# New engine orders for the head and the first ten units of a one-core matmul-tanh-mul kernel, and the sums of one pair and a cast of the next moved later behind them

## The chip, the cores and the metric

One core of a Trainium2 chip. The metric is device time in microseconds (us) of one execution. Every run told of here is of the fast state. Ratios are computed as the mean time of one kernel's fast runs over that of the other's fast runs of the same rounds, so they are not quite the ratio of the medians that are quoted beside them. Engines: PE is TensorE, DVE is VectorE, ACT is ScalarE, SP is the sync engine that issues most DMAs (198 of the 204 that the page of the kernel before lists).

## The reference

```python
batch, m, k, n = 16, 512, 1024, 768        # x: (16, 512, 1024), w1, w2: (1024, 768), float32
y1 = np.matmul(x, w1)
y2 = np.matmul(x, w2)
return (np.tanh(y1) * y2).astype(np.float32)
```

## The kernel before

The 64 x tiles of 128 rows are worked in two ways. The first six tiles ("head") are multiplied directly in bf16 as the weights arrive: matmul `m20F3` is tile 2, weight 0 (called a; weight 1 is b), the wide 512 columns (`G` are the other 256), block 3 of the contraction. The other 58 tiles are 29 pairs. A pair and a weight make a unit of seven fp16 products (four matmuls each) on sums and differences of blocks, instead of eight. DVE and ACT make these sums (`s1` to `s4` of x; `t1` to `t4` and `b11` to `b22` of the weights), scale and cast x (`cx`), and combine products (`c12`, `c22`, seeds, which ACT copies from one bank to another, tanh, final multiply). Fillers are matmuls on a constant tile whose result nobody uses.

The program fixes the order of each engine's instructions. In the traces DVE started its listed casts, blocks, sums, c and multiplies in that order (the first 96 of them, behind which the later units mix in). The orders of the head and of the first ten units stand in the kernel as lists, found by a search; later units are placed by a formula in slots of 0.65 us, one product each.

```python
    FILL = {"m00F0": 3, "m00F1": 6}          # filler matmuls ahead of these two
    ORDER = {
        "pe": """ T00 T01 m00F0 m00G0 T10 T11 m00F1 m00G1 m10F0 T20 ... """,
        "act": """ ... tanh4F tanh5F ax10 ax11 tanh4G ax20 cx11 b11b b22b seed.0 seed.1 ... """,
        "dve": """ ... """, "dma": """ ... """,
    }
    # ... cut ...
    def feed(n, bank=banks[3]):
        for _ in range(n):
            pin(nc.tensor.matmul(bank[:, :2 * P], ones.bitcast(bf16)[:, :P], ones.bitcast(bf16), start=True, stop=True))
    # ... cut ...
    "c12": ("dve", 0.55, 3, ["p3", "u2"], add_out, (u, "d", "u2", "c12")),
    "c22": ("dve", 0.55, 4, ["p7", "s5"], add_out, (u, "b", "s5", "c22")),
    "p4": ("pe", 0.65, 6, ["c22"], unit_product, (u, "p4", "b", False, True)),   # waits for c22
    # ... cut: behind the planned part; FIRST is 6, the seventh pair ...
    for i in range(FIRST, PAIRS):
        z = 14 * i - 6
        at(slot(z - 7), blocks, i)
        for j, n in enumerate(("s1", "s2", "s3", "s4")):
            at(slot(z - 5.5 + 1.3 * j), s_block, i, n, "dve")
        # ... cut ...
        late = 1.1 * (i == FIRST + 1)
        at(slot(z - 25 + late), scale_x, i)
        for h in range(2):
            at(slot(z - 24 + late + 4 * h), cast_x, i, h, "dve")
            at(slot(z - 24 + late + 4 * h), transpose_x, i, h)
```

## Time and profile before

| | before |
|---|---|
| median of the first six runs | 317.22 us (316.65 to 317.68) |
| span of the profiled run | 315.3 us |
| PE, DVE, ACT busy | 98%, 78%, 73% |
| starts that PE loses to waits after 5.12 us | about 2.3 us |

"Starts lost" is the useful measure here: it is the distance between two starts in PE's order of time, less the pace of that shape (0.163 us for 384 columns, from four in 0.65, and 0.216 for 512, from 22 in 4.75, both in the trace of the kernel before). The prediction says why, and shows the lines.

### The profile page before, as it was taken

Reading aid. Unit: us, or ns where it says so; the run is one execution under the profiler, and the core shown is the slowest. Engines: PE = TensorE matmul, PEld = TensorE weight load, DVE = VectorE, ACT = ScalarE, POOL = GpSimd, SP = SyncE. Lnnn points to the kernel's source line nnn. Section 1 sums busy time; section 2 is a strip of 40 time slices with the busy share of each in tenths; the row PEclk is TensorE's granted clock in tenths of the full one; section 3 lists DMA queues with packets and bytes.
Section 4 is the critical chain, followed back from the end, with each engine's and each line's share of the span. In section 5 each row is a group of like instructions: output and inputs, shape, how many; then the busy total and the mean of one; then the engine's idle time right before and its main releaser. Section 6 shows DMA issues by size and latency. Waiting matters only on the chain.

```text
span 315.3 us, 5481 instructions
## 1 busy us (share of the span) xinstructions
PE 307.9 (98%) x1890; PEld 185.5 (59%) x1895; DVE 244.8 (78%) x571; ACT 230.5 (73%) x453; POOL 4.3 (1%) x10
## 2 busy tenths in 40 slices
PE   8999999999998999999999999999999999999994
PEld 5756656666555555555555556555555555555652
DVE  2688978888887778877777897777789777777743
ACT  3788789786887777778777777877777778876551
POOL 0000000000000000000000000000000000000003
PEclk9999999999999999999999999999999999999998
DMA  7999498999999998999999989999998899996222
GB/s 289 406 400 369 95 311 245 262 263 264 308 318 267 287 278 258 246 231 287 268 255 242 285 239 224 299 252 283 242 251 265 263 246 282 234 238 168 101 101 102
DMA packets 82300, 80.59 MB, mean 256 GB/s; under 512 B 63584, under 2 KB 64096, under 8 KB 82272
## 3 DMA queue, kind: packets, MB, share of 16 engines
q1 hardware_dynamic: 81408, 78.27, 89.0%
q10 hardware_dynamic: 864, 1.97, 1.6%
q8 instruction: 15, 0.25, 0.3%
q14 instruction: 13, 0.11, 0.1%
HBM read 39.85 MB, written 25.17 MB: 206 GB/s over the span
## 4 chain that ended last, share of the span: by engine, by line
PE 86%; DMA 6%; DVE 3%; ACT 2%; issue 1%; DVEq 0%; SPq 0%; ACTq 0%
PE bank L401 79%; PE bank L267 4%; DMA x_f<-in_x_dram 3%; DMA xT<-x_h 3%; PE bank L270 2%; PE bank L223 1%; ACT junk L340 1%; DVE x_h L360 1%; DVE o L287 1%; DVE t L318 1%; ACT b L313 0%; DVE c L423 0%; DVE o L437 0%; ACT x_h L362 0%; DVE t L322 0%
## 5 line engine op out<-in xcount | busy, mean ns | idle before, releaser
L401 PE MATMUL bank<-t,s 128*128 128x384 f16 x696 | 131.6, 326 | 0.4 <-DVE t L318 0.4
L401 PEld LDWEIGHTS <-s 128*128 128x128 f16 x928 | 90.6, 98 | 61.1 <-issue 0.8
L401 PEld LDWEIGHTS <-xT 128*128 128x128 f16 x696 | 67.9, 98 | 48.0 <-issue 2.2
L401 PE MATMUL bank<-b,xT 128*128 128x384 f16 x464 | 93.8, 326 | 0.2 <-ACT b L313 0.2
L423 DVE TENSOR_TENSOR c<-bank,u 128x384 f32<-128x384 f32 x58 | 32.0, 554 | 43.6 <-PE bank L401 41.1
L340 ACT ACTIVATE junk<-x_f 128x1024 bf16<-128x1024 f32 x58 | 60.8, 1049 | 2.6 <-DMA x_f<-in_x_dram 2.5
L431 ACT ACTIVATE th<-c,out_r 128x384 f32<-128x384 f32 x58 | 35.3, 609 | 21.9 <-DVE c L423 21.9
L401 PE MATMUL bank<-t,xT 128*128 128x384 f16 x232 | 47.0, 326 | 0.8 <-DVE c L423 0.8
L401 PE MATMUL bank<-b,s 128*128 128x384 f16 x232 | 47.1, 327 | 0.0
L418 ACT ACTIVATE u<-bank 128x384 f32<-128x384 f32 x58 | 28.2, 487 | 19.7 <-PE bank L401 19.3
L360 DVE TENSOR_SCALAR x_h<-x_f,pr 128x1024 f16<-128x1024 f32 x55 | 41.0, 747 | 0.2
L414 ACT ACTIVATE bank<-bank 128x384 f32<-128x384 f32 x58 | 27.8, 481 | 12.7 <-DVE o L437 10.1
L423 DVE TENSOR_TENSOR c<-bank,s 128x384 f32<-128x384 f32 x58 | 32.2, 555 | 6.0 <-PE bank L401 5.0
L431 ACT ACTIVATE th<-bank,out_r 128x384 f32<-128x384 f32 x58 | 33.3, 573 | 4.5 <-PE bank L401 4.5
L437 DVE SCALAR_TENSOR_TENSOR o<-bank,out_r,th 128x384 f32<-128x384 f32 x58 | 35.4, 611 | 0.9 <-PE bank L401 0.9
L437 DVE SCALAR_TENSOR_TENSOR o<-c,out_r,th 128x384 f32<-128x384 f32 (+1 forms) x57 | 34.3, 606 | 0.4 <-ACT th L431 0.2
L418 ACT ACTIVATE s<-bank 128x384 f32<-128x384 f32 x58 | 27.8, 482 | 7.3 <-PE bank L401 5.0
L382 DVE TENSOR_TENSOR s<-xT 128x512 f16<-128x512 f16 x58 | 24.1, 417 | 0.1
L267 PE MATMUL bank<-wb,xTb 128*128 128x512 bf16 x91 | 23.9, 380 | 0.2
L270 PE MATMUL bank<-wb,xTb 128*128 128x256 bf16 x96 | 14.6, 273 | 0.0
L260 ACT ACTIVATE junk<-wf 128x768 bf16<-128x768 f32 (+1 forms) x13 | 12.8, 988 | 1.4 <-DMA wf<-in_w_dram 1.2
L267 PEld LDWEIGHTS <-xTb 128*128 128x128 bf16 x96 | 9.3, 99 | 7.5 <-DVE xTb L231 0.3
(49 smaller groups left out, 144.3 us busy)
## 6 DMA issues: line engine op xcount, KB each, us to landing
x_f<-in_x_dram SPq DMA_DIRECT2D x64, 512.0 KB, 6.0
out_dram<-o SPq DMA_DIRECT2D x62, 384.0 KB, 3.7
wf<-in_w_dram SPq DMA_DIRECT2D x12, 384.0 KB, 8.2
wf<-in_w_dram ACTq DMA_DIRECT2D x4, 384.0 KB, 7.8
xT<-x_h SPq DMA_TRANSPOSE x58, 3.9
out_dram<-o ACTq DMA_DIRECT2D x2, 192.0 KB, 2.1
out_dram<-o SPq DMA_DIRECT2D x2, 192.0 KB, 2.4
```

The source lines that it names most:

```text
L260: pin(nc.scalar.activation(junk[:, :n * N].rearrange("p (k n) -> p k n", n=N), w_f[t][:, k:k + n, :], ACT.Abs, accum_out=asum_w[t][:, j:j ...
L267: pin(nc.tensor.matmul(bank, hx[mt][:, k, :], w_b[t][k][:, :F], start=k == 0, stop=k == KO - 1))
L270: pin(nc.tensor.matmul(bank[:, at_:at_ + G], hx[mt][:, k, :], w_b[t][k][:, F:], start=k == 0 and mt % 2 == 0, stop=k == KO - 1, skip_group ...
L340: pin(nc.scalar.activation(junk[:, :K], xs[HEAD + 2 * i + h], ACT.Abs, scale=2.0 ** -12, accum_out=pair_sum[i][:, h:h + 1]))
L360: pin(nc.vector.tensor_scalar(xh, xs.pop(mt), pair_r[i][:, h:h + 1], None, ALU.mult))
L382: pin((nc.vector if eng == "dve" else nc.gpsimd).tensor_tensor(s, st[i, a], st[i, b], op))
L401: pin(nc.tensor.matmul(bank[:, cols], st[i, a][:, k, :], wt[t][b][:, k, cols], start=start and k == 0, stop=stop and k == KH - 1, skip_gro ...
L414: pin(nc.scalar.activation(ub[u]["b"][:, :Q], ub[u]["a"][:, :Q], ACT.Copy))
L418: pin(nc.scalar.activation(c, ub[u][bank][:, :Q], ACT.Copy))
L423: pin(nc.vector.tensor_tensor(c, ub[u][bank][:, :Q], ub[u][other], ALU.add))
L431: pin(nc.scalar.activation(th, v, ACT.Tanh, scale=rs[i][:, 0, h:h + 1]))
L437: pin(nc.vector.scalar_tensor_tensor(o[:, h, q * Q + cols.start:q * Q + cols.stop], v, rs[i][:, 1, h:h + 1], tanhs[i, h, q][:, cols], ALU. ...
```

## The change

A longer search gave new orders for all engines in the head and the first ten units, and three formulas behind them were shifted. No real work is added or removed; two filler matmuls are added, and some casts and evacuations change their engine. The intent is to remove PE's remaining waits.

```diff
-        "e01": "dve", "e11": "dve", "e20": "act", "e21": "dve", "e31": "dve", "ca0": "act", "ca1": "act",
-        "cb4": "act", "b22a": "dve", "cx11": "act", "cx31": "act", "cx61": "act"
+        "e10": "act", "e21": "dve", "e31": "dve", "cb4": "act", "b22a": "dve", "cx11": "act", "cx31":
+        "act", "cx41": "act", "cx61": "act"
-    FILL = {"m00F0": 3, "m00F1": 6}
+    FILL = {"m00F0": 8, "m10F0": 3}
 PE's list, cut to what matters later:
-   ... suma m11F0 m20F6 m20F7 m01F0 m00G5 m00G6 m00G7 m11F1 m01F1 m30F0 ... m30F7 m21F0 m21F1 m11F2 ...
+   ... suma m20F5 m10G6 m10G7 m30F0 m20F6 m20F7 m11F0 m11F1 m11F2 m01F0 m01F1 m01F2 m31F0 m31F1 m31F2
+   m00F7 m30F1 ... m30F7 m11F3 ...
 ACT's list, cut:
-   ... tanh4F tanh5F ax10 ax11 tanh4G ax20 cx11 b11b b22b seed.0 seed.1 ...
+   ... tanh4F ax10 tanh5F ax11 tanh4G b22b b11b cx11 seed.0 ax21 s5.0 seed.1 u2.0 ax20 ...
 (the rest of the four lists is cut)
-            at(slot(z - 5.5 + 1.3 * j), s_block, i, n, "dve")
+            at(slot(z - 5.5 + 1.6 * (i == FIRST) + 1.3 * j), s_block, i, n, "dve")
-            at(slot(z - 24 + late + 4 * h), cast_x, i, h, "dve")
-            at(slot(z - 24 + late + 4 * h), transpose_x, i, h)
+            at(slot(z - 24 + (1 + h) * late + 4 * h), cast_x, i, h, "dve")
+            at(slot(z - 24 + (1 + h) * late + 4 * h), transpose_x, i, h)
```

More of the change, by code (lines that the diff above doesn't have):

```diff
@@ L58 @@
     ELSEWHERE = {
-        "e01": "dve", "e11": "dve", "e20": "act", "e21": "dve", "e31": "dve", "ca0": "act", "ca1": "act",
-        "cb4": "act", "b22a": "dve", "cx11": "act", "cx31": "act", "cx61": "act"
+        "e10": "act", "e21": "dve", "e31": "dve", "cb4": "act", "b22a": "dve", "cx11": "act", "cx31":
+        "act", "cx41": "act", "cx61": "act"
     }
-    FILL = {"m00F0": 3, "m00F1": 6}
+    FILL = {"m00F0": 8, "m10F0": 3}
     ORDER = {
         "pe": """
-            T00 T01 m00F0 m00G0 T10 T11 m00F1 m00G1 m10F0 T20 m10G0 m10G1 m10F1 T21 m20G0 m20F0 m20F1 m20G1
-            m10G2 m20G2 m00F2 m00G2 m20F2 m10F2 T30 T31 m10G3 m00G3 m20F3 m10F3 m20G3 m00F3 m10F4 m10G4 m20F4
-            m20G4 m00G4 m00F4 m30G0 m30G1 m30G2 m30G3 m20G5 m10G5 m10F5 m20F5 m20G6 m10G6 m10F6 m30G4 m30G5
-            m30G6 m20G7 m10G7 m30G7 m10F7 m00F5 m00F6 m00F7 suma m11F0 m20F6 m20F7 m01F0 m00G5 m00G6 m00G7
-            m11F1 m01F1 m30F0 m30F1 m30F2 m30F3 m30F4 m30F5 m30F6 m30F7 m21F0 m21F1 m11F2 m21F2 m01F2 m11F3
-            m21F3 m01F3 m31F0 m31F1 m31F2 m31F3 m21G0 m21G1 m21G2 m21G3 m31G0 m31G1 m31G2 m31G3 m01F4 m31G4
-            m21G4 m11F4 m01G0 m01G1 m11G0 m11G1 m01G2 m01G3 m01G4 m31F4 T4 m11F5 m11F6 m01F5 m31F5 m01G5 m01G6
-            m31F6 m01F6 m31G5 m31G6 m01F7 m31F7 m11F7 m31G7 T5 m40F0 m40F1 m40F2 m40F3 m40F4 m40F5 m40F6 m01G7
-            m40F7 m21G5 m21G6 m50F0 m50F1 m50F2 m50F3 m50F4 m50F5 m50F6 m50F7 m21F4 m21F5 m21G7 m21F6 m21F7
-            m11G2 m11G3 m11G4 m11G5 m11G6 m11G7 m40G0 m50G0 m50G1 m50G2 m50G3 m50G4 m50G5 m50G6 m50G7 m40G1
-            m40G2 m40G3 m40G4 m40G5 m40G6 m40G7 sumb m41F0 m41F1 m41F2 m41F3 m41F4 m41F5 m41F6 m41F7 m41G0
-            m41G1 m41G2 m41G3 m41G4 m41G5 m41G6 m51G0 m51G1 m51G2 m51G3 m51G4 m51G5 m51G6 m51G7 m41G7 m51F0
-            m51F1 m51F2 m51F3 m51F4 m51F5 m51F6 m51F7 p1.0 p1.1 p5.0 p6.0 p2.0 p3.0 p7.0 p5.1 p6.1 p4.0 p2.1
-            p7.1 p1.2 p3.1 p4.1 p1.3 p6.2 p2.2 p5.2 p6.3 p2.3 p5.3 p7.2 p7.3 p3.2 p4.2 p3.3 p4.3 p1.4 p1.5
-            p5.4 p5.5 p2.4 p6.4 p6.5 p2.5 p7.4 p7.5 p3.4 p3.5 p4.4 p4.5 p1.6 p1.7 p5.6 p6.6 p2.6 p6.7 p2.7
-            p7.6 p3.6 p5.7 p7.7 p4.6 p3.7 p1.8 p4.7 p1.9 p2.8 p6.8 p5.8 p5.9 p7.8 p1.10 p3.8 p4.8 p3.9 p6.9
@@ new lines @@
+            T00 T01 m00F0 m00G0 T10 T11 m10F0 m10G0 m10G1 m00G1 m10F1 m00F1 T20 T21 m00F2 m10G2 m00G2 m10F2
+            m20F0 T30 m20F1 m20G0 m20F2 m20G1 m20G2 T31 m20G3 m20F3 m00G3 m00F3 m10F3 m20G4 m00F4 m10F4 m00G4
+            m20F4 m30G0 m30G1 m30G2 m30G3 m00G5 m00F5 m30G4 m30G5 m20G5 m00F6 m20G6 m00G6 m30G6 m30G7 m20G7
+            m00G7 m10G3 m10G4 m10F5 m10F6 m10F7 m10G5 suma m20F5 m10G6 m10G7 m30F0 m20F6 m20F7 m11F0 m11F1
+            m11F2 m01F0 m01F1 m01F2 m31F0 m31F1 m31F2 m00F7 m30F1 m30F2 m30F3 m30F4 m30F5 m30F6 m30F7 m11F3
@@ new lines @@
+            m11F4 m01F3 m01F4 m31F3 m21G0 m31G0 m21G1 m21G2 m21G3 m21G4 m01G0 m01G1 m01G2 m01G3 m01G4 m11G0
+            m11G1 m21F0 m21F1 m21F2 m21F3 T4 m21F4 m21G5 m01G5 m01G6 m01F5 m11F5 m01F6 m01F7 m21G6 m21G7 m11G2
+            m11G3 m11G4 m11G5 m11G6 m31G1 m31G2 m31G3 m40F0 m40F1 m21F5 m21F6 m21F7 m11F6 m11F7 T5 m31F4 m31F5
+            m31F6 m31F7 m40F2 m40F3 m40F4 m40F5 m40F6 m40F7 m50F0 m50F1 m50F2 m50F3 m50F4 m50F5 m40G0 m40G1
+            m40G2 m50G0 m11G7 m01G7 m50F6 m50F7 m40G3 m40G4 m40G5 m40G6 m40G7 m31G4 m31G5 m50G1 m50G2 m50G3
@@ new lines @@
+            m50G4 m50G5 m50G6 m50G7 sumb m41F0 m41F1 m41F2 m41F3 m41F4 m41F5 m41F6 m41F7 m31G6 m31G7 m41G0
+            m41G1 m51G0 m41G2 m41G3 m41G4 m41G5 m41G6 m41G7 m51G1 m51G2 m51G3 m51G4 m51G5 m51G6 m51G7 m51F0
+            m51F1 m51F2 m51F3 m51F4 p1.0 p1.1 p5.0 p2.0 p6.0 p5.1 m51F5 m51F6 p6.1 p7.0 p3.0 p7.1 p4.0 m51F7
+            p3.1 p2.1 p4.1 p1.2 p1.3 p5.2 p5.3 p6.2 p2.2 p6.3 p2.3 p7.2 p7.3 p3.2 p4.2 p3.3 p4.3 p1.4 p1.5
+            p5.4 p6.4 p2.4 p2.5 p6.5 p5.5 p7.4 p7.5 p3.4 p4.4 p3.5 p4.5 p1.6 p1.7 p5.6 p5.7 p6.6 p2.6 p6.7
@@ L81 @@
+            p2.7 p7.6 p7.7 p3.6 p4.6 p3.7 p4.7 p1.8 p1.9 p5.8 p6.8 p2.8 p5.9 p7.8 p1.10 p3.8 p4.8 p3.9 p6.9
             p2.9 p2.10 p7.9 p5.10 p4.9
@@ L83 @@
         "act": """
-            ca0 absa0 ca1 absa1 e20 absa2 absa3 absa4 absa5 absa6 absa7 tanh2G absb0 tanh1F tanh0G tanh2F cb4
-            tanh0F absb2 absb6 tanh3F absb4 ax00 absb7 ax01 b21a tanh4F tanh5F ax10 ax11 tanh4G ax20 cx11 b11b
-            b22b seed.0 seed.1 s5.0 u2.0 ax21 b21b u2.1 f00.0 s5.1 f10.0 ax31 seed.2 ax30 seed.3 f11.0 u2.2
-            u2.3 s5.2 s5.3 f00.2 f01.0 ax40 cx31 f10.2 seed.4 ax41 seed.5 s5.4 s5.5 u2.4 u2.5 f11.2 f00.4 ax51
-            f01.2 ax50 f10.4 seed.6 f11.4 seed.7 f01.4 u2.6 s5.6 ax61 u2.7 s5.7 f00.6 f11.6 f10.6 seed.8 ax60
@@ L89 @@
-            f00.8 u2.8 f01.6 s5.8 cx61 s5.9 seed.9 f10.8 seed.10 u2.9 f01.8 f11.8 f00.10 s5.10
+            e01 absa0 e10 e11 absa1 absa2 absa3 absa4 absa5 absa6 absa7 tanh2G absb0 tanh0G b21a cb4 tanh2F
+            tanh0F tanh1F absb2 absb4 absb7 tanh3F ax00 ax01 absb6 tanh4F ax10 tanh5F ax11 tanh4G b22b b11b
+            cx11 seed.0 ax21 s5.0 seed.1 u2.0 ax20 u2.1 s5.1 b21b f00.0 f10.0 ax31 f11.0 f01.0 seed.2 seed.3
+            ax30 u2.2 u2.3 s5.2 s5.3 f00.2 ax41 f10.2 ax40 seed.4 cx31 seed.5 u2.4 f01.2 f11.2 u2.5 s5.4 s5.5
@@ L90 @@
+            f00.4 ax51 cx41 f10.4 seed.6 f01.4 ax50 seed.7 f11.4 u2.6 u2.7 s5.6 s5.7 f00.6 ax61 f11.6 f10.6
+            seed.8 ax60 f01.6 u2.8 f00.8 s5.8 s5.9 cx61 seed.9 f10.8 seed.10 u2.9 f01.8 f11.8 f00.10 s5.10
         """,
         "dve": """
-            e00 e01 e10 e11 ca2 e21 ca3 ca4 e30 ca5 ca6 e31 ca7 parta cb0 cb1 scalea b11a cb2 cb3 t1a b22a hx4
-            cb6 cb5 t2a e41 cb7 hx5 mul0F mul3F mul1F e51 t3a rx0 cx00 cx01 mul2G mul2F mul0G partb t4a rx1
-            cx10 scaleb mul4F sx0 mul4G s1.0 s2.0 s4.0 s3.0 sx1 t1b t2b t3b c22.0 rx2 sx2 cx20 t4b s1.1 c22.1
@@ L95 @@
-            f00.1 s2.1 c12.0 f10.1 s3.1 cx21 c12.1 s4.1 f11.1 rx3 cx30 c22.2 c22.3 s3.2 s1.2 f00.3 f01.1 c12.2
-            c12.3 s2.2 f10.3 mul5F rx4 cx40 s4.2 cx41 s3.3 c22.4 f11.3 c22.5 f00.5 s1.3 c12.4 f01.3 s2.3 f10.5
-            rx5 f11.5 s4.3 cx50 c12.5 f01.5 c22.6 sx3 cx51 c22.7 f00.7 s1.4 s2.4 sx4 s3.4 c12.6 c12.7 rx6 cx60
-            s4.4 sx5 f01.7 c22.8 f10.7 f11.7 s1.5 s2.5 c12.8 s3.5 c12.9 f00.9 c22.9 s4.5 f11.9 f01.9 f10.9
+            e00 ca0 ca1 ca2 e20 e21 ca3 ca4 e30 ca5 e31 ca6 ca7 cb0 parta cb1 scalea cb2 b22a cb3 b11a t1a t2a
@@ new lines @@
+            hx4 cb5 cb6 cb7 e41 mul0F hx5 t3a t4a mul1F e51 rx0 cx00 mul3F partb mul2F mul0G cx01 scaleb sx0
+            rx1 cx10 mul4F mul2G mul4G s1.0 s3.0 s2.0 t1b t2b s4.0 t3b rx2 c22.0 cx20 c22.1 t4b s1.1 f00.1
+            c12.0 c12.1 f10.1 s2.1 cx21 sx1 s3.1 s4.1 rx3 cx30 f11.1 c22.2 c22.3 s1.2 mul5F f00.3 c12.2 s2.2
+            s4.2 f10.3 rx4 f01.1 c12.3 s3.2 sx2 cx40 f11.3 c22.4 c22.5 s1.3 f00.5 c12.4 f01.3 c12.5 s2.3 s4.3
+            f10.5 s3.3 f01.5 rx5 cx50 s3.4 f11.5 sx3 c22.6 c22.7 cx51 f00.7 sx4 s1.4 c12.6 s2.4 s4.4 c12.7
@@ L99 @@
+            f11.7 rx6 cx60 f01.7 c22.8 f10.7 c12.8 s1.5 s2.5 s4.5 s3.5 sx5 f00.9 c12.9 c22.9 f01.9 f10.9 f11.9
         """,
         "dma": """
-            Lx0 La0 Lx1 La1 Lx2 La2 Lx3 La3 La4 La5 La6 La7 Lb0 Lb1 Lb2 Lb3 Lb4 Lx4 Lb5 Lb6 Lx5 Lb7 Lp00 Lp01
-            Lp10 Lp11 Tx00 Lp20 Tx01 st3 Lp21 Tx10 Lp30 st4 Tx11 Lp31 st1 Tx20 Lp40 Lp41 Tx21 st2 Lp50 Tx30
-            Lp51 Tx31 Lp60 st5 Tx40 Lp61 st0 Tx41 Lp70 store1.5 Tx50 store0.5 Lp71 Tx51 store0.1 store1.1 Tx60
+            Lx0 La0 Lx1 La1 Lx2 La2 Lx3 La3 La4 La5 La6 La7 Lb0 Lb1 Lb2 Lb3 Lb4 Lx4 Lb5 Lx5 Lb6 Lb7 Lp00 Lp01
@@ L104 @@
+            Lp10 Lp11 Tx00 Lp20 Tx01 Lp21 st0 Tx10 st4 Lp30 Tx11 Lp31 Tx20 Lp40 Lp41 Tx21 Lp50 st1 Tx30 st5
+            Lp51 Tx31 store0.1 st3 Tx40 Lp60 st2 Tx41 Lp61 store0.5 Tx50 Lp70 store1.5 Tx51 store1.1 Lp71 Tx60
             store0.7 store1.7 Tx61 store1.3 store0.3 store0.9 store1.9
```

## The prediction

> **What bounds the kernel now.** I read the page first, then the list of PE's waits, then PE, DVE and ACT in order of time around each wait, and last the chain. The page says that PE has next to no idle time:
>
> ```profile
> PE 307.9 (98%) x1890; PEld 185.5 (59%) x1895; DVE 244.8 (78%) x571; ACT 230.5 (73%) x453; POOL 4.3 (1%) x10
> PE   8999999999998999999999999999999999999994
> PEclk9999999999999999999999999999999999999998
> L401 PE MATMUL bank<-t,s 128*128 128x384 f16 x696 | 131.6, 326 | 0.4 <-DVE t L318 0.4
> ```
>
> The 98% alone proves little, because ends of matmuls are modelled. So I check the pace: in the lines of PE in order of time, a product of four 128x384 matmuls starts every 0.65 us (93.09, then 93.74), 162.5 ns a matmul, although one lasts 326 ns in the row. There are 29 pairs of x blocks by two weights, 58 units of 7 products: 406 x 0.65 = 263.9 us. The first part, six x tiles by direct bf16 matmuls, has 96 matmuls of 512 columns and 96 of 256, starting 0.216 and 0.109 us apart (22 in 4.75, 8 in 0.87 in the chain): 31.2 us. Eight fp32 transposes of four blocks at 0.60 are 4.8, two bf16 ones about 1.0, nine filler matmuls about 1.0 (six took 0.66), two sums 0.3. Together 302.2 us. PE starts the first transpose at 5.12 and ends at about 309.5, so 304.4 us hold 302.2 of work: about 2.2 us can be won by any order, 0.7% of the time. All waits of PE after the first one, which only holds the warm-up matmuls, are these:
>
> ```profile
> PE bank L401 <- DVE c L423: 0.8, 1, 0.8
> PE bank L401 <- DVE t L318: 0.4, 1, 0.4
> PE bank L401 <- ACT b L313: 0.2, 1, 0.2
> PE bank L223 <- DMA x_f<-in_x_dram: 0.2, 1, 0.2
> ```
>
> These are counted after the modelled end, which lies 0.16 past the next possible start (0.81 long against a pace of 0.65). In lost starts they are larger. PE in order of time, columns start and length:
>
> ```profile
> 43.19 0.81 PE L401 MATMUL bank<-b,xT 128*128 128x384 f16 x4
> 44.25 0.81 PE L401 MATMUL bank<-b,xT 128*128 128x384 f16 x4 [0.25 <-ACT b L313]
> 44.90 0.81 PE L401 MATMUL bank<-t,s 128*128 128x384 f16 x4
> 46.09 0.81 PE L401 MATMUL bank<-t,s 128*128 128x384 f16 x4 [0.38 <-DVE t L318]
> ...
> 95.04 0.81 PE L401 MATMUL bank<-b,xT 128*128 128x384 f16 x4
> 96.70 0.81 PE L401 MATMUL bank<-t,xT 128*128 128x384 f16 x4 [0.84 <-DVE c L423]
> ```
>
> 44.25 - 43.19 - 0.65 = 0.41; 46.09 - 44.90 - 0.65 = 0.54; 96.70 - 95.04 - 0.65 = 1.01. The early one, for the second x tile, is 7.54 - 7.07 - 0.11 = 0.36. Sum 2.32 us, which fits the 2.2 from the other side. The largest is on VectorE's order, as DVE in order of time shows:
>
> ```profile
> 94.29 0.43 DVE L382 TENSOR_TENSOR s<-xT 128x512 f16<-128x512 f16 x1
> 94.63 0.55 DVE L423 TENSOR_TENSOR c<-bank,u 128x384 f32<-128x384 f32 x1
> 95.10 0.75 DVE L360 TENSOR_SCALAR x_h<-x_f,pr 128x1024 f16<-128x1024 f32 x1
> 95.75 0.42 DVE L382 TENSOR_TENSOR s<-s,xT 128x512 f16<-128x512 f16 x1
> 96.09 0.55 DVE L423 TENSOR_TENSOR c<-bank,s 128x384 f32<-128x384 f32 x1
> ```
>
> The product at 96.70 needs the second c, which stands behind a sum, a cast and another sum that nobody needs yet. The chain adds that the first sum had itself waited for a transpose that landed at 94.27:
>
> ```profile
> 87.97 6.29 DMA xT<-x_h
> 94.27 0.02 issue
> 94.29 0.04 DVE s L382
> ```
>
> After 96.70 the chain is one piece of PE, 212.80 us with 1300 matmuls, and then a tail of some 6 us that the change leaves alone.
>
> [...] a ready c stands 1.1 us behind work that isn't urgent.[...] the granted clock is 1.00 in every stretch of the first 300 us,[...] so no clock effect is at stake.[...]
>
> **The change part by part.** No kind of real work is added or removed. The order of instructions grows by four rows on PE, two filler matmuls with their weight loads (3 + 6 becomes 8 + 3): 2 x 0.11 = +0.22 us where PE is otherwise dense. Two weight casts move from ACT (0.83 each) to DVE (0.56), and two evacuations of the first transposes from DVE (0.69) to ACT (0.58).
>
> (a) Start. First evacuation 6.09 to 6.74 as now, then the first weight cast on DVE to about 7.3, while the longer filler runs to about 7.2; first matmul about 7.4, where it is 6.84 now. The second tile's transposes no longer find PE empty at 7.2 to 7.54; they run about 7.7 to 8.8. Then the order catches up: by my count from the durations both kernels have the transposes of tiles 0 to 2 and eight matmuls behind them at about 11.2 to 11.3. Gain of the wait 0.36, cost of fillers 0.22: -0.14 net.
>
> (b) Middle of the first part. The second weight's last two loads now come behind the last head tile, so the cast of load 6 moves by about 1.3 us (512 KB at 400 GB/s). Counting forward with the durations of now, it ends near 27.4 and its matmul comes near 28.0; the last cast ends near 28.4, its use near 28.7. No wait, slack 0.3 to 0.6. Zero.
>
> (c) The passage at 43 to 46. Today ACT idles 1.90 us on a load of x before 40.55, then does its abs, a cast of x (1.13) and only then the two weight blocks of 1.5 us; the second product waits for the first block, a later one for t (1.82 on DVE) or the seed that ACT copies at 45.58. In the new order that abs comes later and both blocks stand ahead of the cast of x. From the second sum near 38.1: scale ready 38.9, blocks done 40.5 and 42.0; t from about 43.9 to 45.7. The first products start near 43.0, the one with t near 46.2 because other products and two head matmuls stand ahead. So 0.41 + 0.54 = 0.95 can vanish, but slacks are 0.3 to 0.9 us and ACT still meets a load at about 44. I count half: -0.5.
>
> (d) The rest of the ten units has no wait now and cannot gain, but its order is new. For waits that appear here or in (b) I allow +0.4.
>
> (e) Behind the planned part. The four sums of that pair go 1.6 slots (1.04 us) later and the second cast 1.1 slots (0.7) later. In the built order both c stand directly ahead of sum and cast. The first c can then start near 94.2 and the second near 94.8, done by 95.4, before 95.69. The 1.01 vanishes; nothing hurries the sums, as the product that uses the first one follows about 4 us later. At 9 chances in 10: -0.9.
>
> Sum: -0.14 - 0.5 + 0.4 - 0.9 = -1.1 us.
>
> **The rivals.** First, a wait replaces a wait: the new order of the first ten units was made from planned durations, as the present one was, and that one shows 1.3 us of lost starts in the first 46 us. For it speak slacks of 0.3 us and transposes that land 3.0 to 6.7 us after issue; against it that between 46.7 and 95 the present one has none. Then only (e) remains, or less: 316.5 to 317.5. Second, everything fits: 2.32 - 0.22 = 2.1 us saved, 315.1; that is the floor. Third, a late transpose or load blocks a FIFO engine for several us, as that of 6.29 us nearly did; two or three such would make 319 to 321. Stores in the queue of the same issuing engine have moved ahead of some transposes, which speaks for it; the 4 us and more between landing and use speak against it.
>
> **Range and chances.** 317.2 - 1.1 gives 316.1 us. The floor sets the low end, 315.1; giving back all of (c) and a new wait of about a microsecond sets the high end, 317.4. Faster by 2% needs 6.3 us, three times all waits there are: 1%. Slower by 2% needs new stalls of as much: 2%.
>
> **What would show it.** Right if PE's list of waits loses the one for c at 96.70 and DVE shows both c ahead of the sum there; if blocks b on ACT begin near 39 and no start is lost near 43 to 46; if PE from 96 on is still one piece. Wrong if PE waits appear between 46 and 90 or on a transpose, if two c still wait, if the clock falls, or if the tail changes by itself.

That the products cannot go faster was the author's estimate; the trace of the kernel before shows that none of its 1624 matmuls of 384 columns starts less than 0.161 us after the one before it, with 0.162 as the median. The 400 GB/s of (b) are near what the same trace shows: 395, 407 and 413 in the windows from 15 to 20, 20 to 25 and 25 to 30. For the third rival, the list of SP's waits there has 7.2 us as the longest at a store (L452).

## The result, and the profile after

316.89 us median (316.47 to 317.31, six runs) against 317.22; ratio 0.999, interval 0.9977 to 1.0003. Beside other kernels in a later session the same two kernels gave 317.11 and 317.53, ratio 0.9981 (0.9966 to 0.9996). So the gain is one to two parts in a thousand, clear of noise only in the second comparison. The range held; the middle of it, 316.1, did not: about a third of the expected 1.1 us came.

The page of the changed kernel looks like the one before. In its group rows the waits have other names: those for t and b are gone from the 384-column rows, the one for c is smaller, and the head's wide matmuls show a new one:

```profile
PE 308.2 (98%) x1897; PEld 186.0 (59%) x1897; DVE 243.8 (77%) x570; ACT 230.9 (73%) x454; POOL 4.3 (1%) x10
L401 PE MATMUL bank<-t,s 128*128 128x384 f16 x696 | 131.3, 326 | 0.0
L401 PE MATMUL bank<-t,xT 128*128 128x384 f16 x232 | 47.1, 325 | 0.4 <-DVE c L423 0.4
L267 PE MATMUL bank<-wb,xTb 128*128 128x512 bf16 x96 | 25.1, 379 | 0.9 <-DVE wb L254 0.9
```

The list of PE's waits says it in four lines (us in total, times, longest); the first is the start and the same as before; the last, for x, now stands at 5.22, ahead of the first tile:

```profile
PE bank L153 <- DVE ones L155: 1.0, 1, 1.0
PE bank L267 <- DVE wb L254: 0.9, 2, 0.6
PE bank L401 <- DVE c L423: 0.4, 1, 0.4
PE bank L223 <- DMA x_f<-in_x_dram: 0.2, 1, 0.2
```

PE in order of time (start, length), at the old places and the new ones:

```profile
18.74 1.03 PE L267 MATMUL bank<-wb,xTb 128*128 128x512 bf16 x4
20.11 0.38 PE L267 MATMUL bank<-wb,xTb 128*128 128x512 bf16 x1 [0.35 <-DVE wb L254]
21.06 4.48 PE L267 MATMUL bank<-wb,xTb 128*128 128x512 bf16 x20 [0.57 <-DVE wb L254]
...
43.53 1.46 PE L401 MATMUL bank<-b,xT 128*128 128x384 f16 x8
44.83 0.81 PE L401 MATMUL bank<-t,s 128*128 128x384 f16 x4
45.48 0.81 PE L401 MATMUL bank<-b,xT 128*128 128x384 f16 x4
...
95.18 0.81 PE L401 MATMUL bank<-b,xT 128*128 128x384 f16 x4
95.83 0.81 PE L401 MATMUL bank<-t,xT 128*128 128x384 f16 x4
...
104.38 0.81 PE L401 MATMUL bank<-b,xT 128*128 128x384 f16 x4
105.59 0.81 PE L401 MATMUL bank<-t,xT 128*128 128x384 f16 x4 [0.40 <-DVE c L423]
```

From 43.53 to 46.13 the products follow each other at 0.65 without a gap, and so they do at 95.18 and 95.83: the three old waits are gone. New ones stand at 20.11 (four starts after 18.74 the next was due at 19.60: 0.51 lost), at 21.06 (0.73 lost) and at 105.59 (0.56 lost).

What VectorE did at these two new places:

```profile
17.43 0.15 DVE L297 TENSOR_REDUCE tot<-asum_w 128x1 f32<-128x8 f32 x1
19.50 0.56 DVE L254 CAST wb<-wf 128x768 bf16<-128x768 f32 x1 [1.92 <-DMA wf<-in_w_dram]
19.97 0.15 DVE L347 TENSOR_SCALAR w_inv<-bank 128x1 int32<-128x1 int32 x1
20.16 0.15 DVE L348 TENSOR_SCALAR w_inv<-w_inv 128x1 f32<-128x1 f32 x1
20.35 0.16 DVE L350 RECIPROCAL wp0r<-w_inv 128x1 f32<-128x1 f32 x1
20.44 0.56 DVE L254 CAST wb<-wf 128x768 bf16<-128x768 f32 x1
...
103.85 0.42 DVE L382 TENSOR_TENSOR s<-xT 128x512 f16<-128x512 f16 x1 [0.43 <-DMA xT<-x_h]
104.19 0.55 DVE L423 TENSOR_TENSOR c<-bank,u 128x384 f32<-128x384 f32 x1
104.66 0.41 DVE L382 TENSOR_TENSOR s<-s,xT 128x512 f16<-128x512 f16 x1
104.99 0.55 DVE L423 TENSOR_TENSOR c<-bank,s 128x384 f32<-128x384 f32 x1
```

At 19.50 the cast of load b1 had waited 1.92 us for its load. At 103.85 a sum waited for a transposed block, and both c, needed at once, stood behind it: the same picture that the kernel before shows at 94.29, one pair later. The chain, which before ran through the passage at 46 and the transpose at 88, now runs through these two DMAs:

```profile
10.55 8.92 DMA wf<-in_w_dram
...
97.59 6.23 DMA xT<-x_h
```

The account in starts lost, from the matmuls' starts of the two traces (us):

| place | before | after |
|---|---|---|
| second x tile, 7.1 | 0.37 | none (the fillers fill it) |
| casts of b1 and b2, near 20 | none | 0.51 + 0.73 |
| passage at 43 to 46 | 0.41 + 0.54 | none |
| c near 96 | 1.01 | none |
| c near 105 | none | 0.56 |
| sum | 2.33 | 1.80 |

Two more fillers cost 0.22, and the same set of transposes and head matmuls ends at 11.00 in place of 11.14. With -0.14 for that stretch, +1.24 - 0.95 - 1.01 + 0.56 make -0.30 us. Medians say -0.33, spans -0.2.

### The profile page after: what moved, and what is told of

It is laid out like the page before. It is cut to its first block, busy times and chain, and to the rows that moved or that the text cites. A ratio compares the mean times of both kernels' runs of the same rounds, so it can differ in the third digit from the quotient of the medians.

```text
span 315.1 us, 5484 instructions
## 1 busy us (share of the span) xinstructions
PE 308.2 (98%) x1897; PEld 186.0 (59%) x1897; DVE 243.8 (77%) x570; ACT 230.9 (73%) x454; POOL 4.3 (1%) x10
## 4 chain that ended last, share of the span: by engine, by line
PE 89%; DMA 8%; DVE 1%; issue 0%; ACTq 0%; DVEq 0%; SPq 0%
PE bank L401 82%; DMA wf<-in_w_dram 6%; PE bank L267 5%; PE bank L270 2%; DMA xT<-x_h 2%; DVE c L423 0%; DVE o L437 0%; DVE wb L254 0%; PE bank L238 0%; ACTq L250 0%; DVEq L749 0%; DVE s L382 0%; SPq L250 0%; DVE wp0r L350 0%; DVE w_inv L348 0%
## 5 line engine op out<-in xcount | busy, mean ns | idle before, releaser
L360 DVE TENSOR_SCALAR x_h<-x_f,pr 128x1024 f16<-128x1024 f32 x54 | 40.3, 746 | 0.2
L267 PE MATMUL bank<-wb,xTb 128*128 128x512 bf16 x96 | 25.1, 379 | 0.9 <-DVE wb L254 0.9
L270 PE MATMUL bank<-wb,xTb 128*128 128x256 bf16 x96 | 13.7, 272 | 0.0
```

What stands on the lines that cost most here:

```text
L267: pin(nc.tensor.matmul(bank, hx[mt][:, k, :], w_b[t][k][:, :F], start=k == 0, stop=k == KO - 1))
L270: pin(nc.tensor.matmul(bank[:, at_:at_ + G], hx[mt][:, k, :], w_b[t][k][:, F:], start=k == 0 and mt % 2 == 0, stop=k == KO - 1, skip_group ...
L360: pin(nc.vector.tensor_scalar(xh, xs.pop(mt), pair_r[i][:, h:h + 1], None, ALU.mult))
```

## The experiments

All kernels gave correct results. Each was timed in five rounds beside the kernel before on the same chip. None differs from the kernel before by 2%; the intervals show which smaller differences are clear of noise.

| kernel | median us | before, same session | ratio, 95% interval |
|---|---|---|---|
| tail_only | 316.80 | 317.35 | 0.9983 (0.9946 to 1.0020) |
| orders_only | 317.79 | 317.35 | 1.0008 (0.9975 to 1.0040) |
| first_b_later | 316.07 | 317.35 | 0.9948 (0.9918 to 0.9977) |
| sums2_tail | 316.02 | 317.35 | 0.9949 (0.9915 to 0.9983) |
| both_fixes | 315.43 | 317.45 | 0.9941 (0.9915 to 0.9966) |
| wide_fill | 317.03 | 317.45 | 0.9974 (0.9951 to 0.9996) |
| narrow_fill | 317.20 | 317.45 | 0.9987 (0.9963 to 1.0010) |
| act_blocks_first | 317.50 | 317.45 | 0.9999 (0.9969 to 1.0029) |
| wide_sums2 | 315.39 | 317.53 | 0.9929 (0.9915 to 0.9943) |
| both_no_fill | 316.38 | 317.53 | 0.9957 (0.9940 to 0.9973) |
| after_again | 317.11 | 317.53 | 0.9981 (0.9966 to 0.9996) |
| both_again | 315.65 | 317.53 | 0.9943 (0.9924 to 0.9961) |

My theory after the result: both parts of the change do what they were made for, and both hand part of it on to a new wait. The new PE order asks for the casts of b1 and b2 before their loads land, and the tail's part moves a late transpose's wait to the next pair. The rival for the first: the head is bound by its loads as a whole, so any order waits as much. The rival for the second: the tail's part does nothing.

### The tail's part alone, and the orders alone

tail_only is the kernel before with the three shifted lines; orders_only is the changed kernel with these lines as before.

```diff
 tail_only, against before:
-            at(slot(z - 5.5 + 1.3 * j), s_block, i, n, "dve")
+            at(slot(z - 5.5 + 1.6 * (i == FIRST) + 1.3 * j), s_block, i, n, "dve")
-            at(slot(z - 24 + late + 4 * h), ...)
+            at(slot(z - 24 + (1 + h) * late + 4 * h), ...)
 orders_only, against after: the same lines the other way round
```

> The first ten units of the kernel before with only the new places of the sums and the cast behind them. Theory A (the tail's part works and merely passes a smaller wait to the next pair): PE's 0.84 us wait for c near 96.7 is gone, a wait of about 0.4 us (0.56 in starts) for c stands near 105.5 behind a sum that waits for a late transpose; time 316.8 (0.5 us under the kernel before). Rival (the tail's part does nothing by itself, the new orders made the wait go): a wait near 96 of 0.8 stays, time as before, 317.2. If the whole first wait is saved with nothing behind: 316.2.

> The new orders of the first ten units with the old places of sums and cast. Theory A: the waits for the second weight's casts near 20 (0.35 and 0.57) stay, no waits at 43 to 46, and a wait for c of about 0.8 comes back near 96; the orders alone are worth 2.3 - 1.0 - 1.23 - 0.22 - some 0.4, about nothing: time 317.2 to 317.5, same as the kernel before. Rival (the orders are a gain of half a microsecond and more and the tail ate it): 316.4 or less.

tail_only: the wait near 96 is gone from the trace, and the wait near 105 that I expected is not there (0.09 us lost). Its late block landed at 102.87, in the changed kernel at 103.83. The whole microsecond was kept in that trace, and the waits at 43 to 46 stayed (0.34 and 0.55), as they should; the timed gain of 0.55 us agrees in sign but is not clear of noise. So by the trace the second rival falls, and in this execution nothing was handed on to the next pair.

orders_only: PE waits for c at its old place, and longer than in the kernel before (98.62 - 96.33 - 0.65 = 1.64 us of starts):

```profile
96.33 0.81 PE L401 MATMUL bank<-b,xT 128*128 128x384 f16 x4
98.62 0.65 PE L401 MATMUL bank<-t,xT 128*128 128x384 f16 x3 [1.47 <-DVE c L423]
```

So in these two traces the tail's part is worth 1.64 - 0.56 = 1.1 us with the new orders, and without it the new orders alone show no gain. My expectation missed in three points: the time is above 317.2 to 317.5, the wait for c is twice the expected one, and the waits near 20 are not in this trace. Its first x tile landed at 6.02 us instead of 5.1, PE then ran at half pace for a while (see the end of the part on why the prediction was right or wrong), and the first matmul on b1 started at 21.99 where the changed kernel's was due at 19.60; b1 had landed at 18.84 and b2 at 19.81, so the loads were in time. That profiled run took 319.0 us, more than its kernel's median of 317.79, so its other times are not typical.

### First weight ahead of b1 and b2

```diff
-   m30F0 m20F6 m20F7 m11F0 m11F1 m11F2 m01F0 m01F1 m01F2 m31F0 m31F1 m31F2 m00F7 m30F1 ... m30F7 m11F3
-   m11F4 m01F3 m01F4 m31F3 m21G0
+   m30F0 m20F6 m20F7 m11F0 m01F0 m00F7 m30F1 ... m30F7 m11F1 m11F2 m01F1 m01F2 m31F0 m31F1 m31F2 m11F3
+   m01F3 m31F3 m11F4 m01F4 m21G0
```

> The changed kernel with one edit of PE's order: the eight matmuls of the first weight that need nothing new run ahead of the second weight's matmuls on its loads 1 and 2. Theory A (the new PE order asks for these two casts about 1.2 us before their loads land): both waits for a cast near 20 are gone, 1.23 us of lost starts, of which later loads and casts (of load 4 on ACT, of head tile 4) may take back up to 0.6; time 315.7 to 316.4. Rival (the first part is bound by its loads as a whole, so that the wait only moves to a later cast): as much is lost between 23 and 30, time 316.9 as the changed kernel.

316.07 us. In PE's order of time 25 wide matmuls now follow each other without a wait, 5.4 us from the first start to that of the next group, where the changed kernel waits twice:

```profile
18.79 5.56 PE L267 MATMUL bank<-wb,xTb 128*128 128x512 bf16 x25
24.19 1.58 PE L270 MATMUL bank<-wb,xTb 128*128 128x256 bf16 x13
```

The only loss that followed is 0.18 us before a transpose at 26.65. So the first rival falls: the loads left room, the order had not used it. The wait for c near 105 stayed (0.52).

### Sums of the next pair later too

```diff
-            at(slot(z - 5.5 + 1.6 * (i == FIRST) + 1.3 * j), s_block, i, n, "dve")
+            at(slot(z - 5.5 + 1.6 * (i <= FIRST + 1) + 1.3 * j), s_block, i, n, "dve")
```

> The changed kernel with the sums of the next pair also 1.6 slots later. Theory A (the new wait near 105 is c standing behind a sum that waits for the transposed block of the cast that was moved): both c of that unit stand ahead of the sum, no wait near 105, 0.56 us saved, time 316.3. Rival (the transpose lands so late that the wait moves on to a product that needs the sum or the block): a wait of 0.3 or more between 106 and 110, time 316.9.

316.02 us, and no PE wait for c; the wait for the cast of b2 stayed (0.98 us of starts at 20.91). Its transposed block landed at 103.83, no earlier than in the changed kernel, but both c now stand ahead of the sum that needs it:

```profile
103.21 0.56 DVE L423 TENSOR_TENSOR c<-bank,u 128x384 f32<-128x384 f32 x1
103.79 0.56 DVE L423 TENSOR_TENSOR c<-bank,s 128x384 f32<-128x384 f32 x1
104.27 0.42 DVE L382 TENSOR_TENSOR s<-xT 128x512 f16<-128x512 f16 x1
```

In this trace the late transpose harmed nobody; the order had made it harmful. Why this transpose took 5.0 to 8.0 us in the fourteen traces, and the one issued near 88 took 6.3 to 7.9, was not examined.

### Both edits

> The changed kernel with both edits of the first round (the first weight's matmuls ahead of the second weight's loads 1 and 2; the sums of the next pair later too). If the two waits are independent, the savings add: against the kernel before 0.9948 and 0.9949 were measured for each, with 0.999 for the change alone, so 0.991: about 314.8 to 315.6, and no wait of PE for a cast near 20 nor for c near 105. Rival (one chain paces both, the later one is only hidden by the earlier): no better than the better of the two, 316.0.

> Both edits once more, to compare with the changed kernel on one chip: 315.4, no waits of PE after the start; 1.4 to 1.6 under the changed kernel.

315.43, and 315.65 in another session, there 1.5 us under the changed kernel's 317.11. In the first trace the list of PE's waits has a single line, the start (the second has one more, 1.2 us for the first x, which landed at 5.88 instead of 5.05):

```profile
PE bank L153 <- DVE ones L155: 1.0, 1, 1.0
```

By the ratios (0.9941 and 0.9943, against 0.9948 and 0.9949 for either edit alone, intervals overlapping) it is not shown that the two savings add; one of the first six runs took 317.42, and five lie between 315.34 and 315.68. That both waits are gone is shown by the traces. The floor of the prediction was 315.1.

### Why the loads b1 and b2 land late

In the raw records (of the packed trace, which no view prints) each load signals sixteen times. For b1 in the changed kernel the first signal comes at 17.50, the fifteenth at 17.91 and the last at 19.47; for the load before it the first and last come at 16.52 and 16.93. So most of the transfer is in time and a last part is 1.5 us late, and so it is for the loads that follow. In the same records one DMA packet of 16 KB, of a queue that the page calls instruction, starts at 17.29 and takes 1.09 us. The page counts 15 packets on that queue. These packets go with PE's instructions: between two of them the trace lists 253 of PE on average (matmuls and weight loads, 3794 in all; ACT has about 600 listed in the whole kernel, DVE about 720), and in all fourteen traces the first of them starts when 203 to 217 of these have started, at times from 13.29 to 19.85. So I took them for the fetch of PE's own instructions, an inference that the next two runs test. To test what it does I changed the number of PE instructions ahead of it, not the time that they take.

```diff
 wide_fill, against after: fillers two by two (3766 PE instructions in place of 3794)
-        for _ in range(n):
-            pin(nc.tensor.matmul(bank[:, :2 * P], ones.bitcast(bf16)[:, :P], ones.bitcast(bf16), ...))
+        for m in [2] * (n // 2) + [1] * (n % 2):
+            pin(nc.tensor.matmul(bank[:, :m * 2 * P].rearrange("p (a b) -> p a b", a=m), ones.bitcast(bf16)[:, :P],
+                                 ones.bitcast(bf16).unsqueeze(1).to_broadcast([P, m, 2 * P]), ...))
 narrow_fill, against after: each filler in two halves (58 PE instructions more)
+        for _ in range(2 * n):
+            pin(nc.tensor.matmul(bank[:, :P], ones.bitcast(bf16)[:, :P], ones.bitcast(bf16)[:, :P], ...))
```

> The changed kernel with its filler matmuls two by two in one of 512 columns: the same PE time, 28 instructions fewer on PE ahead of everything. Theory F (the loads fall 1.3 us behind because PE's own instructions are fetched[...] at about 17.4, one 16 KB packet of 1.1 us, and the loads from then on wait for it): the fetch comes later, about 19 to 20; loads 1 and 2 of the second weight land near 18.0 and 19.0 in place of 19.5 and 20.4, the late landings begin at load 3; both waits near 20 go; time 315.7 to 316.2. Rival (the loads fall behind at a fixed time or amount of data, whatever PE fetches): landings and waits as in the changed kernel, 316.9.

> The changed kernel with each filler matmul split in two of 128 columns: about the same PE time, 58 instructions more on PE ahead of everything. Theory F: the fetch comes some 3 us earlier, about 14, and the late landings (first step to last over 1.5 us) begin with load 6 or 7 of the first weight, or the first of the second; waits for casts of as much or more than now in the first 21 us, time 316.9 to 318. Rival: landings late from load 1 or 2 of the second weight on as now, time 316.9.

From the DMA records (start of the 16 KB packet; last signal of loads; first load whose last signal is over 1.5 us behind its first):

| kernel | packet at | b1 landed | b2 landed | late from |
|---|---|---|---|---|
| narrow_fill | 13.29 | 19.25 | 20.24 | a6 |
| after | 17.29 | 19.47 | 20.42 | b1 |
| first_b_later | 17.32 | 17.95 | 20.23 | b2 |
| after_again | 17.42 | 18.05 | 20.30 | b2 |
| before | 17.48 | 18.14 | 20.24 | b2 |
| wide_fill | 19.34 | 17.86 | 18.83 | b4 |
| wide_sums2 | 19.85 | 18.09 | 19.11 | b4 |

The packet moves with PE's instruction count and the lateness moves with the packet, in both directions. That settles the cause of the late part. The amount is not constant: in these seven kernels the last signal came 1.1 to 1.6 us behind the fifteenth, in orders_only only 0.13, where the first and last signals had been 1.3 us apart before the packet too. It also says that the kernel before had the late b2 (20.24) in plain sight; its PE order only did not ask for it. In after_again b1 is in time and b2 late, and PE loses 1.00 us once instead of 0.51 and 0.73.

wide_fill lost both waits near 20, as expected, and narrow_fill got waits for casts at 16.9 and 17.9 in their place (0.73 and 0.47 us of starts):

```profile
16.91 0.38 PE L267 MATMUL bank<-wb,xTb 128*128 128x512 bf16 x1 [0.56 <-DVE wb L254]
...
17.92 0.27 PE L270 MATMUL bank<-wb,xTb 128*128 128x256 bf16 x1 [0.30 <-DVE wb L254]
```

narrow_fill has no wait near 105; it lost 0.80 us at 79.25 instead, on a c behind a sum for which DVE had stood idle 2.07 us until a transpose landed: the same picture at a third pair.

But wide_fill's time missed my expectation: 317.03, not 315.7 to 316.2. PE came to the place near 104 more than a microsecond sooner, the block landed at 103.82 (103.83 in the changed kernel), and the wait for c grew from 0.56 to 1.65 us of starts:

```profile
101.58 0.75 DVE L361 TENSOR_SCALAR x_h<-x_f,pr 128x1024 f16<-128x1024 f32 x1
103.84 0.42 DVE L383 TENSOR_TENSOR s<-xT 128x512 f16<-128x512 f16 x1 [1.51 <-DMA xT<-x_h]
104.19 0.55 DVE L424 TENSOR_TENSOR c<-bank,u 128x384 f32<-128x384 f32 x1
```

DVE stood still for 1.5 us with the two c behind the sum. This landing is not fixed: the block was issued at 95.95, 1.6 us sooner than in the changed kernel (97.59), and fifteen of its sixteen signals were there at 102.30. A 16 KB packet of PE's fetch started at 101.20 and took 1.51 us. wide_sums2 shows the same (102.83, last signal 104.33, packet at 101.52). So the fetch that the wide fillers moved off the loads may have struck this block; but in both_no_fill a packet at 101.24 left the block's signals together (104.06 to 104.16), and no run tests it. One run of the six took 315.70, so the wait may be missing in some executions. If this account is whole, the later sums must bring the gain back:

```diff
 wide_sums2, against wide_fill
-            at(slot(z - 5.5 + 1.6 * (i == FIRST) + 1.3 * j), s_block, i, n, "dve")
+            at(slot(z - 5.5 + 1.6 * (i <= FIRST + 1) + 1.3 * j), s_block, i, n, "dve")
```

> The changed kernel with wide fillers and with the sums of the next pair 1.6 slots later. Wide fillers alone took both waits near 20 away and yet were no faster, as one wait for c near 104 grew to 1.65 us of starts behind the sum that waits for a transpose. If that is the whole account: no such wait, time as with both edits, 315.3 to 315.8. Rival (with loads in time, PE is simply ahead of a transpose that its products need, whatever VectorE's order): a wait of a microsecond and more stays near 104 to 108, 316.9.

315.39 us, all five runs between 314.99 and 315.47, ratio 0.9929: the steadiest version, and with both_fixes (315.43) the fastest.

### The passage at 43 to 46, by itself

```diff
 act_blocks_first, against before
-   tanh4F tanh5F ax10 ax11 tanh4G ax20 cx11 b11b b22b seed.0 seed.1
+   tanh4F tanh5F ax10 ax11 tanh4G b11b b22b ax20 seed.0 cx11 seed.1
```

> The kernel before with one edit of ACT's order: the second weight's two blocks ahead of the abs and the cast of x that waits for a load, and the seed ahead of that cast. Theory of the prediction (the passage at 43 to 46 loses 0.41 and 0.54 us of starts because these blocks stand behind that abs): both waits (for b, 0.25, and for t, 0.38) go, the wait near 96 stays; time 316.3 to 316.5. Rival (the passage is bound by something else, the scale of the second weight or VectorE's t): the wait for t stays at 0.3 or more, or one of the same size follows within some us; time 317.0 or more.

The waits at 43 to 46 went, so ACT's order was their cause. A new one for ACT's seed came at 54.38, 0.42 us of starts:

```profile
43.56 1.46 PE L401 MATMUL bank<-b,xT 128*128 128x384 f16 x8
44.86 1.46 PE L401 MATMUL bank<-t,s 128*128 128x384 f16 x8
...
53.31 0.81 PE L401 MATMUL bank<-b,xT 128*128 128x384 f16 x4
54.38 0.81 PE L401 MATMUL bank<-t,s 128*128 128x384 f16 x4 [0.25 <-ACT bank L414]
```

By the trace half a microsecond is left; by the time, 317.50 against 317.45 and an expected 316.3 to 316.5, nothing is seen. Its runs spread from 316.44 to 318.92, and the first x tile of the profiled one landed at 5.68. Whether the half microsecond is real stays open.

### No fillers

```diff
 both_no_fill, against both_fixes
-    FILL = {"m00F0": 8, "m10F0": 3}
+    FILL = {}
```

> Both edits, and no filler matmuls after the warm-up ones. If the eleven fillers run only while PE would wait for x or a cast anyhow (as the traces of the changed kernel suggest at 6.6 to 7.5 and 8.7 to 9.1): same time within 0.3, 315.2 to 315.7, and the clock stays at full. If each costs its 0.11 us as the prediction had it for the two added ones: 1.2 us less, 314.3.[...] The fetch of PE's instructions should come about a microsecond later, near 18.5.

Median 316.38, six runs from 315.43 to 316.74, against 315.65 with fillers in the same session. That is above the expected 315.2 to 315.7. PE idles where they stood (0.97 and 0.40 us of starts before the first matmul and the second tile's) and is no further ahead afterwards (the matmul behind the third tile's transposes starts 5.48 us after the first transpose, 5.43 with fillers). So here a filler in a wait for data costs nothing, and taking all away gains nothing. The clock stayed at full from 3.77 on, so in this trace these fillers weren't needed for it. The fetch moved to 19.82, later than the 18.5 that I expected. Why the median is higher rather than equal isn't settled; the intervals of the two ratios overlap, and the median spans are closer, 314.1 against 313.8.

### The changed kernel again

> The changed kernel itself, beside the others on this chip: 316.9, the waits near 20 (0.9 in all, for casts of the second weight's loads 1 and 2, or 0.8 for load 2 alone if the instruction fetch falls a load later) and the wait near 105 (0.4) as in its first trace.

317.11 us. The wait near 105 was 1.24 us of starts in this trace, with the block landing at 104.39; it was 0.56 in the first, with 103.83. So it varies from run to run with that landing.

## Why the prediction was right or wrong, point by point

The range (315.1 to 317.4) and the chances held: no order can win 2% where PE has 2.3 us of waits. Holding the range says little, for it reaches from every wait saved to a small loss; and errors of opposite sign in (b) and (c) met in the sum. The limit from counting starts was close; both_fixes and wide_sums2 came to about 0.3 us of the floor, and two single runs went below it (314.99 and 315.08). The other count, 302.2 us of work, agreed in part by luck: it took four fp32 transposes at 0.60, but at full clock their starts are 0.11 apart (eight in 0.88, from 10.12 to 11.00 in the changed kernel), so the work is some 1.3 us less and more could be won than 2.2.

The central sum, -1.1 us, was too large by 0.8. By its terms:

- (a) Start, -0.14: the stretch ended 0.14 earlier. Right. Its pricing of the two fillers at 0.22 was formally right in the sum, but they sit in PE's wait for x and the first casts and cost nothing of themselves (both_no_fill).
- (b) Middle of the first part, "Zero": this is the term that failed. I followed the loads 6 and 7 of the second weight, which the new DMA order moves, and did not set the new PE order against the landings of loads 1 and 2, which it asks for 0.4 us (load 1, due at 19.60 in place of 20.04) and 2.8 us (load 2, due at 19.82 in place of 22.63) earlier than the old one. Measured: 1.24 us. The landing of b2 at 20.24 was in the kernel before's records.
- (c) Passage at 43 to 46, half of 0.95: all of it went. ACT began the two blocks at 39.52, about half a microsecond after the 39 of the prediction, and no start was lost. Too cautious by 0.45.
- (d) +0.4 for new waits in (b) or later in the ten units: none came later in the ten units beyond a piece of 0.15 us at 87.88; in (b) the size was a third of the true one.
- (e) Behind the planned part, -0.9: the 1.01 went, as both c stand ahead of sum and cast. The statement that nothing hurries the sums held for that pair. It did not go on to the pair whose cast was moved: 0.56 us came back there. So the term is -0.45. The third rival (a late transpose holds what stands behind it) was named with the wrong argument against it: microseconds between landing and use of a block do not help c, which stands behind the sum in the queue.

Of its own signs, "PE from 96 on is still one piece" failed, at 105.59. In the prediction's first rival, "a wait replaces a wait", lies most of what happened, twice: near 20 in place of 43 to 46, near 105 in place of 96.

One reading was too trusting. "The granted clock is 1.00 in every stretch" comes from a view that has no record ahead of the first change of the clock. In orders_only's trace the record begins at 10.25 us (5.77 in the kernel before): after an idle 1.10 us for a late first x, matmuls started at half pace until then (fillers 0.21 us apart in place of 0.11), while the view read 1.00 there too. PE had started again at 6.16, so full pace came 4.1 us later. In both_again and both_no_fill full pace had begun at 4.38 and 3.77, and idle times of 1.2 and 1.3 us after that did not end it. So in these traces such an idle went with half pace only where full pace had not yet begun.

The landing of the very first load varies: 4.94 to 6.02 us over the profiled runs, a wider span than the change's gain. What it costs the whole time isn't shown; with both edits a first x at 5.88 instead of 5.05 went with a first product at 43.04 instead of 42.59.

## What to carry to other kernels

Before moving work ahead on the bounding engine, list when each input actually landed in the trace, last part included, and set every new first use against it; a load that was late without harm becomes a wait as soon as the order asks for it (b2 landed at 20.24 in the kernel before without harm, at 20.42 in the changed one, where PE lost 0.73 us to its cast). On an engine that works in the given order, as DVE's traces show here, put what the bounding engine waits for ahead of anything that may itself wait for a DMA: a late transpose cost up to 1.65 us here because two urgent additions stood behind a sum that nobody needed yet. Remove waits one behind the other in one version before judging any of them, for a later wait can swallow the time that an earlier one gave (wide_fill 317.03, with the later wait removed 315.39).
